# One transformer block in fp32 on one core: the two ends of the feed-forward rearranged, and the planner's estimate for one-pass products made shorter

## The chip, the cores and the metric

The kernel runs on one core of a Trainium2 chip. Its time is the device time of the whole program in microseconds (us). A core has engines that each take their instructions strictly in the order in which they were written: TensorE (PE in the profile, with its weight loads as PEld), VectorE (DVE), ScalarE (ACT), GpSimd (POOL), and queues that start DMA transfers (SP's above all). An engine waits on semaphores until what its next instruction reads is there, and everything behind that instruction waits too.

## The reference

One layer on 512 tokens of width 1024, all in fp32: a token mixer of four groups, attention to 256 memory rows, and a feed-forward of width 2816, each with a root-mean-square norm before it and another behind it.

```python
for l in range(DEPTH):                       # DEPTH = 1
    h = token_mixer(rmsnorm(x, norm_mix_pre[l]), ...)
    x = x + rmsnorm(h, norm_mix_post[l])
    h = memory_cross_attention(rmsnorm(x, norm_cross_pre[l]), rmsnorm(mem, mem_norm[l]), ...)
    x = x + rmsnorm(h, norm_cross_post[l])
    h = conv_glu_ffn(rmsnorm(x, norm_ffn_pre[l]), w_ffn_in[l], ffn_conv_w[l], ffn_conv_b[l], w_ffn_out[l])
    x = x + rmsnorm(h, norm_ffn_post[l])

def conv_glu_ffn(xn, w_up, conv_w, conv_b, w_down):
    gu = xn @ w_up
    gate, up = jnp.split(gu, 2, axis=-1)
    gate = causal_dwconv(gate, conv_w) + conv_b.astype(gate.dtype)
    return (jax.nn.silu(gate) * up) @ w_down
```

## The kernel before

**Products.** Each large fp32 product runs as three one-pass matmuls of a type called fp32r (`three`): high part by high part, low by high, high by low. `split` makes the parts: ScalarE copies the high part (`xTh`, `wh`, `sh`, `hh` ...), VectorE subtracts it from the value for the low part (`xTl`, `wl`, `sl`, `hl` ...). A "group" below is one such three of matmuls.

**Who orders the work.** Nothing is issued as the code is read. Every operation goes to a list scheduler (`Plan`), which knows a cost for it, what it depends on, and how many SBUF slots and PSUM banks (8) there are. It walks through an estimated time, takes the operation that can start first, and among those within 1 ns the one with the longest estimated rest of the program (`bl`) plus a `boost` written at the call. What comes out is one fixed list for each engine. The estimate for a matmul is `mcost`; it costs no time on the chip and acts only through the order.

**Feed-forward, first end.** After the attention to memory, each of four row tiles t of 128 tokens is normalized (`norm_T`: `xs` on VectorE, eight transposes on TensorE, then `xTh` and `xTl`). For t = 2 and 3 the transposed tile is also kept unsplit (`xf`, "keep"), and differences of kept tiles (t=2 with 0, 3 with 1) are split into `Th` and `Tl`.

**The 22 column tiles f.** The product with `w_ffn_in` is made for tiles of 128 gate and 128 up columns. Six tiles, `PLAIN`, are done by `plain`: two products of 8 groups, 512 columns wide. For f = 0 each product is made in two halves of 256 columns (tokens of t = 0, 1, and of t = 2, 3), so that the first halves need only row tiles 0 and 1. The other 16 are done by `seven`, a scheme with seven smaller products (S1, S3, G1, S2, S4, U2, G2) of 12 matmuls of 256 columns, on sums and differences of weight blocks made in `blocks` by VectorE (`su`, `st`) and split by ScalarE (`wh`, `uh`, `sh`) and VectorE (`wl`, `sl`, `ul`). Their results are put together again from the copies `c57`, `c1` (both named c in the rows) and `gu`; then `glu` (convolution, Silu, product) gives `hT`.

**Feed-forward, last end.** `hh` and `hl` are the parts of `hT` for the product with `w_ffn_out`. `down(f, t, c)` is one group of 512 columns; eight accumulators `od[t][c]` stand in all eight banks, and f runs in the outer loop, the last three f per row tile. What may not start before the end of the 22 tiles is tied to `up_`, the last tile's U2 product.

Of the kernel before, what the change touches and what calls it, by code (L numbers as in the profile page):

```python
# [22 lines left out]
AF = mybir.ActivationFunctionType  # L23
# [3 lines left out]
P = 128  # L27
S = 512
D = 1024
# [1 line left out]
NT = S // P  # L31
DFF = 2816
NF = DFF // P
PLAIN = (0, 1, 2, 6, 11, 16)
EPS = 1e-6
NEG = -1e30

# [305 lines left out]
def kernel(  # L343
# [108 lines left out]
    def mcost(l, n):  # L452
        m = min(l.size(), P)
        if l.buf.dt == FR:
            return max(n, 2 * m) * 0.4445 + 3.7
        return max(n, m) / 0.6 + 4.8

    def mms(o, terms, first=True, last=True, spare=0, n=None, quota=(), after=(), boost=0.0, fifo=None, cold=1, open_=False):
# [113 lines left out]
    @unit  # L572
    def norm_T(src, g, dst, keep=None):
        xs = [sb([P, 512], FT, "xs") for _ in range(2)]
        r = rms([src[:, h * 512:(h + 1) * 512] for h in range(2)], xs)
        for h in range(2):
            hs = slice(h * 512, (h + 1) * 512)
            stt(xs[h].all, src[:, hs], r[:, 0:1], g[:, hs], OP.mult, OP.mult)
        for h in range(2):
            p = ps([P, 4, P])  # L580
            for k in range(4):
                tpose(p[:, k, :], xs[h][:, k * P:(k + 1) * P], idn)
            if keep:
                act(keep[h], p.all, AF.Copy)
            split(*dst(h), p.all)

    def into(t):
        return lambda h: (xTh[:, t, 4 * h:4 * h + 4], xTl[:, t, 4 * h:4 * h + 4])
# [509 lines left out]
    for t in range(NT):  # L1098
        pl.boost = -5000.0 * t
        qh, ql = qT[t // 2]  # L1100
        tq = slice((t % 2) * P, (t % 2) * P + P)
        oh_, ol_ = sb([P, 4, P], FR, "oh"), sb([P, 4, P], FR, "ol")
        for hp in range(2):
            with pl.unit():
                sp, mx, pr = ps([P, 2, 256]), sb([P, 4], FT, "cmx"), sb([P, 2, 256], FT, "cpr")
                for hh in range(2):
                    h = hp * 2 + hh
                    mms(sp[:, hh, :], three(qh[:, h, tq], ql[:, h, tq], ckh[:, h, :], ckl[:, h, :]), n=256)
                rmax(mx[:, 0:2], sp.all)
                ts(mx[:, 0:2], mx[:, 0:2], -CS, None, OP.mult)  # L1110
                for hh in range(2):
                    act(pr[:, hh, :], sp[:, hh, :], AF.Exp, bias=mx[:, hh:hh + 1], scale=CS,
                        accum=mx[:, 2 + hh:3 + hh])
                recip(mx[:, 2:4], mx[:, 2:4])
                tt(pr.all, pr.all, mx[:, 2:4, None].bc([P, 2, 256]), OP.mult)
                tp, pt = ps([P, 2, 2, P]), sb([P, 2, 2, P], FT, "cpt")
                for hh in range(2):
                    for m in range(2):
                        tpose(tp[:, hh, m, :], pr[:, hh, m * P:(m + 1) * P], idn)
                act(pt.all, tp.all, AF.Copy)  # L1120
                oT = ps([P, 2, P])
                for hh in range(2):
                    h = hp * 2 + hh
                    mms(oT[:, hh, :], [(cv[:, m, h * P:(h + 1) * P], pt[:, hh, m, :]) for m in range(2)])
                split(oh_[:, 2 * hp:2 * hp + 2, :], ol_[:, 2 * hp:2 * hp + 2, :], oT.all)
        with pl.unit():
            pp = []
            for c in range(2):
                p, cs = ps([P, 512]), slice(c * 512, c * 512 + 512)
                for k in range(4):  # L1130
                    wh, wl = wo[k]
                    mms(p.all, three(oh_[:, k, :], ol_[:, k, :], wh[:, 0, cs], wl[:, 0, cs]), k == 0, k == 3,
                        spare=BIG)
                pp.append(p)
            xo2 = residual(pp, g_cpost, t)
        if t < 2:
            xf.append([sb([P, 4, P], FT, "xf") for h in range(2)])
            norm_T(X[t], g_fpre, into(t), [b.all for b in xf[t]])
        else:
            with pl.unit():  # L1140
                b1, b2 = [sb([P, 4, P], FT, "xf") for h in range(2)]
                norm_T(X[t], g_fpre, into(t), [b1.all, b2.all])
                a1, a2 = xf[t - 2]
                i = t - 2
                pl.boost -= 60000.0

                tt(a1.all, b1.all, a1.all, OP.subtract)
                tt(b1.all, b2.all, b1.all, OP.subtract)
                tt(b2.all, b2.all, a1.all, OP.subtract)
                tt(a2.all, a2.all, b2.all, OP.subtract)  # L1150
                for j, v in enumerate((a1, b2, b1, a2)):
                    split(Th[j][:, i], Tl[j][:, i], v.all)
                pl.boost += 60000.0
        kept.append(store(flat(x2, t * P * D, [[D, P], [1, D]]), X[t].all, P * D * 4))


# [18 lines left out]
    def plain(f):  # L1175
        ww = [stage(wsrc(w_ffn_in, 0, KT, j * DFF + f * P, P), [P, KT, P], 8 if f < 2 else 4) for j in range(2)]
        with pl.unit():
            pp = []
            for j in range(2):
                p = ps([P, S])  # L1180
                wh, wl = ww[j]
                for hv_ in [slice(0, 2), slice(2, 4)] if f < 1 else [slice(0, 4)]:
                    for k in range(KT):
                        o = mms(p[:, hv_.start * P:hv_.stop * P],
                                three(wh[:, k, :], wl[:, k, :], xTh[:, hv_, k, :], xTl[:, hv_, k, :]),
                                k == 0, k == KT - 1)
                pp.append(p)
            glu(f, pp[0], pp[1].all)
        return o

    def raw(f):
        with pl.unit():
# [48 lines left out]
    def seven(f):  # L1241
        W = blocks(*raw(f))
        with pl.unit():
            a, b = ps([P, 2, 256]), ps([P, 2, 256])

            def prod(o, w, xs, first):
                return mms(o, [q for i in range(4) for q in three(W[w][0][i], W[w][1][i], *xs[i])], first, n=256, open_=True)
            prod(b[:, 0], "S1", tblock(0), True)
            prod(b[:, 1], "S3", tblock(2), False)
            prod(a[:, 0], "G1", xblock(0, 0), True)  # L1250
            prod(a[:, 1], "S2", tblock(1), False)
            c57 = sb([P, 2, 256], FT, "c57")
            act(c57.all, b.all, AF.Copy)
            prod(b[:, 0], "S4", xblock(1, 1), False)
            o = prod(b[:, 1], "U2", tblock(3), False)
            c1 = sb([P, 256], FT, "c1")
            act(c1.all, a[:, 0], AF.Copy)
            prod(a[:, 0], "G2", xblock(1, 0), False)
# [4 lines left out]
            tt(c57[:, 0], c57[:, 0], c57[:, 1], OP.add)  # L1263
            tt(gu[:, 768:], c1.all, c57[:, 0], OP.add)
            glu(f, gu, gu[:, S:])
        return o

    ups = [plain(f) if f in PLAIN else seven(f) for f in range(NF)]
    up_ = ups[-1]

    g_fpost = gain(norm_ffn_post, [up_])
    NL = 3
    wd, hT = [], []
    for f in range(NF):
# [6 lines left out]
            wd.append((hb.all, lb2.all))  # L1281
        with pl.unit():
            hh, hl = sb([P, S], FR, "hh", kind="hh"), sb([P, S], FR, "hl")
            act(hh.all, hP[f // 2][:, f % 2, :], AF.Copy, quota=[("hh", 4)], after=[ups[-2]])
            tt(hl.all, hP[f // 2][:, f % 2, :], hh.all.cast(FT), OP.subtract)
            hT.append((hh, hl))

# [6 lines left out]
    od = [[ps([P, 512]) for c in range(2)] for t in range(NT)]  # L1294
    for t in range(NT):
        X[t] = sb([P, D], FT, "X2")
        load(X[t].all, flat(x2, t * P * D, [[D, P], [1, D]]), P * D * 4, after=[kept[t], up_])
    for f in range(NF - NL):
        with pl.unit():
            for t in range(NT):  # L1300
                for c in range(2):
# [121 lines left out]
```

## Time and profile before

| what | us |
|---|---|
| median of 3 runs | 748.5 (746.23 to 749.05) |
| the profiled execution | 747.11 |
| its span, first to last instruction | 745.3 |
| TensorE busy in it | 727.7 (98%) |
| VectorE busy | 522.6 (70%) |
| ScalarE busy | 389.1 (52%) |

The times are read on one profiled execution; start times in it are us from the span's start. TensorE's busy time counts overlapping matmuls by their union, so that a matmul listed with 0.39 us may start 0.23 us after the one before it: the distance between two starts is what one costs in a stream. In the rows, `[0.79 <-DVE xs L412]` behind an instruction says that its engine stood idle for 0.79 us before it and which engine's result ended that. The feed-forward's 22 tiles lie between 382 and 616 us, the product with `w_ffn_out` between 616 and 739 us.

### The profile page before, as it was taken

What the parts mean: (1) busy time and instruction counts of PE and PEld (TensorE: products, weight loads), DVE (VectorE), ACT (ScalarE), POOL (GpSimd) and SP (SyncE); (2) the same over time, 40 slices, a digit from 0 to 9 for tenths busy, and PEclk for the clock granted to TensorE, in tenths of its full rate; (3) what the DMA queues carried; (4) which work ended last, traced back from release to release, by engine and by line L of the source; (5) the groups of instructions that cost most, each with busy time, mean ns of one, the idle gap of its engine ahead of it and who ended that gap; (6) DMA issues with size and microseconds to landing.
All of it is one profiled execution on the core that took longest, in us unless ns stands there. A gap on an engine that the chain in (4) does not pass through costs nothing.

```text
span 745.3 us, 11908 instructions
## 1 busy us (share of the span) xinstructions
PE 727.7 (98%) x4614; PEld 647.4 (87%) x4614; DVE 522.6 (70%) x1007; ACT 389.1 (52%) x790; POOL 35.5 (5%) x65
## 2 busy tenths in 40 slices
PE   7999999999999999999999999999999989999996
PEld 6898989998887988889887999999999988888885
DVE  5889956785674646676888679898979997334105
ACT  6794347546574545465666355463655565324102
POOL 3000210011000001000010000000000000000001
PEclk9999999999999999999999999999999999999999
DMA  8800320410325543333134043052234146441003
GB/s 300 299 1 1 130 93 29 173 55 28 112 116 163 163 155 103 123 113 121 51 118 166 29 142 114 29 179 77 77 126 134 34 161 235 141 150 49 0 1 113
DMA packets 25696, 82.07 MB, mean 110 GB/s; under 512 B 2980, under 2 KB 4644, under 8 KB 25640
## 3 DMA queue, kind: packets, MB, share of 16 engines
q1 hardware_dynamic: 25352, 80.72, 31.9%
q8 instruction: 36, 0.59, 0.3%
q0 software_dynamic: 288, 0.59, 0.3%
q14 instruction: 20, 0.16, 0.1%
HBM read 77.10 MB, written 4.20 MB: 109 GB/s over the span
## 4 chain that ended last, share of the span: by engine, by line
PE 85%; DVE 7%; ACT 5%; issue 2%; DMA 1%; POOL 0%; SPq 0%; DVEq 0%; POOLq 0%; ACTq 0%
PE p L462 81%; PE p L479 3%; DMA st<-in_w_in_dram 1%; PE p L474 1%; ACT wh L387 1%; DVE at L428 1%; DVE wl L400 1%; DVE Qt L400 0%; ACT e L387 0%; POOL rr L565 0%; DVE xTl L400 0%; DVE X L412 0%; DVE pg L400 0%; DVE E L400 0%; DVE sl L400 0%
## 5 line engine op out<-in xcount | busy, mean ns | idle before, releaser
L462 PE MATMUL p<-xTh,wh 128*128 128x512 f32 (+1 forms) x432 | 147.4, 341 | 2.5 <-ACT c L387 2.0
L462 PE MATMUL p<-xTl,wh 128*128 128x512 f32 (+1 forms) x432 | 145.7, 337 | 0.7 <-DVE xTl L400 0.7
L462 PE MATMUL p<-xTh,wl 128*128 128x512 f32 (+1 forms) x432 | 145.3, 336 | 0.0
L400 DVE TENSOR_TENSOR wl<-st,wh 128x1024 fp32r<-128x1024 f32 (+3 forms) x101 | 118.7, 1190 | 29.8 <-ACT wh L387 29.7
L387 ACT ACTIVATE wh<-st 128x1024 fp32r<-128x1024 f32 (+3 forms) x101 | 101.5, 1029 | 8.5 <-DMA st<-in_w_in_dram 5.8
L462 PEld LDWEIGHTS p<-xTh,wh 128*128 128x128 f32 x432 | 81.7, 189 | 10.8 <-ACT c L387 2.4
L462 PEld LDWEIGHTS p<-xTh,wl 128*128 128x128 f32 x432 | 81.7, 189 | 9.3
L462 PEld LDWEIGHTS p<-xTl,wh 128*128 128x128 f32 x432 | 81.8, 189 | 8.4 <-DVE xTl L400 1.1
L462 PE MATMUL p<-wh,xTh 128*128 128x256 f32 (+1 forms) x192 | 56.5, 294 | 0.2 <-ACT xTh L387 0.2
L462 PE MATMUL p<-wh,hh 128*128 128x512 f32 x144 | 56.7, 394 | 0.0
L462 PE MATMUL p<-wh,hl 128*128 128x512 f32 x144 | 56.7, 394 | 0.0
L462 PE MATMUL p<-wl,hh 128*128 128x512 f32 x144 | 56.7, 394 | 0.0
L462 PE MATMUL p<-wh,xTl 128*128 128x256 f32 (+1 forms) x192 | 54.0, 281 | 0.4 <-DVE xTl L400 0.4
L462 PE MATMUL p<-wl,xTh 128*128 128x256 f32 (+1 forms) x192 | 54.1, 282 | 0.0
L462 PE MATMUL p<-Th,sl 128*128 128x256 f32 x192 | 54.0, 281 | 0.0
L462 PE MATMUL p<-Th,sh 128*128 128x256 f32 x192 | 53.9, 281 | 0.0
L462 PE MATMUL p<-Tl,sh 128*128 128x256 f32 x192 | 53.9, 281 | 0.0
L400 DVE TENSOR_TENSOR hl<-hT,hh 128x512 fp32r<-128x512 f32 x22 | 15.1, 690 | 52.8 <-ACT hh L387 52.8
L387 ACT ACTIVATE hh<-hT 128x512 fp32r<-128x512 f32 x22 | 13.8, 629 | 64.2 <-PE p L462 64.2
L565 POOL TENSOR_TENSOR rr<-rv,mhalf 128x1 f32<-128x1 f32 x26 | 15.8, 608 | 568.5 <-DVE rv L407 565.0
L462 PEld LDWEIGHTS p<-wh,xTh 128*128 128x128 f32 x192 | 36.2, 189 | 1.0 <-ACT xTh L387 0.5
L400 DVE TENSOR_TENSOR pg<-p,gain 128x512 f32<-128x512 f32 x24 | 16.4, 685 | 29.1 <-ACT sq L387 29.1
(281 smaller groups left out, 1760.9 us busy)
## 6 DMA issues: line engine op xcount, KB each, us to landing
st<-in_w_ffn_in_dram SPq DMA_DIRECT2D x44, 512.0 KB, 4.5
st<-in_w_in_dram SPq DMA_DIRECT2D x24, 512.0 KB, 4.3
st<-in_w_ffn_out_dram SPq DMA_DIRECT2D x22, 512.0 KB, 3.7
st<-in_w_mix_out_dram SPq DMA_DIRECT2D x8, 512.0 KB, 4.6
st<-in_w_ck_dram SPq DMA_DIRECT2D x4, 512.0 KB, 9.1
st<-in_w_cv_dram SPq DMA_DIRECT2D x4, 512.0 KB, 3.9
X<-in_x_dram SPq DMA_DIRECT2D x4, 512.0 KB, 3.9
st<-in_w_cq_dram SPq DMA_DIRECT2D x4, 512.0 KB, 3.9
```

The lines of the kernel that those rows point to most:

```text
L387: return nc.scalar.activation(o.ap(), i.ap(), func, **kw)
L400: return pl.op(eng, c, lambda: e.tensor_tensor(o.ap(), a.ap(), b.ap(), op=op), reads=[a, b], writes=[o], fifo=fifo, boost=boost)
L428: return pl.op("DVE", dcost(n, True), lambda: nc.vector.copy_predicated(o.ap(), m.ap(), a.ap()), reads=[m, a, o], writes=[o])
L462: i = nc.tensor.matmul(o.ap(), l.ap(), r.ap(), start=first and j == 0, stop=last and j == len(terms) - 1, skip_group_check=open_)
L474: i = nc.tensor.matmul(o[hh * 64:hh * 64 + 64].ap(), l.ap(), r.ap(), start=j == 0, stop=j == len(terms) - 1)
L479: return pl.op("PE", 109.0, lambda: nc.tensor.transpose(o.ap(), a.ap(), idn.ap()), reads=[a, idn], writes=[o])
L565: pl.op("Pool", 470.0, lambda: nc.gpsimd.tensor_tensor(r.all.ap(), v.all.ap(), mhalf[:, :1].ap(), op=OP.pow), reads=[v.all, mhalf.all], wr ...
```

## The change

- Of the six plain tiles, f = 16 becomes f = 17.
- `mcost` for fp32r goes from 231.3 to 215.7 ns for 512 columns and from 117.5 to 109.1 ns for 256 (the two formulas at n = 512 and 256): an estimate, which can only change orders.
- In `norm_T` the split is written ahead of the keep copy. The norm before the feed-forward gets a boost of 5000, and the differences of kept tiles one of -60000 alone.
- `plain` halves its products for f = 0 and f = 1. For f = 1 this takes away 16 groups of 512 columns and adds 32 of 256: 96 matmuls in place of 48.
- `plain` and `seven` return two operations. For the last tile these are its S1 product (`up_`) and its U2 product (`upe`). The `hh` copies wait for S1 of the last tile where they waited for the tile before it (U2 of f = 20); the gain and the loads of `X2` wait for U2 of the last tile as before.
- The eight `down` groups of f = 0 leave the common unit, become units of their own, and may start once S1 of the last tile is done.

```diff
-PLAIN = (0, 1, 2, 6, 11, 16)
+PLAIN = (0, 1, 2, 6, 11, 17)
...
         if l.buf.dt == FR:
-            return max(n, 2 * m) * 0.4445 + 3.7
+            return max(n, 2 * m) / 2.4 + 2.4
...
+            split(*dst(h), p.all)
             if keep:
                 act(keep[h], p.all, AF.Copy)
-            split(*dst(h), p.all)
...
+        pl.boost = 5000.0
         if t < 2:
...
-                pl.boost -= 60000.0
+                pl.boost = -60000.0
...
-                pl.boost += 60000.0
...
-                for hv_ in [slice(0, 2), slice(2, 4)] if f < 1 else [slice(0, 4)]:
+                for hv_ in [slice(0, 2), slice(2, 4)] if f < 2 else [slice(0, 4)]:
...
-            prod(b[:, 0], "S1", tblock(0), True)
+            o = prod(b[:, 0], "S1", tblock(0), True)
...
-            o = prod(b[:, 1], "U2", tblock(3), False)
+            e = prod(b[:, 1], "U2", tblock(3), False)
...
-        return o
+        return o, e
...
-    up_ = ups[-1]
-
-    g_fpost = gain(norm_ffn_post, [up_])
+    up_, upe = ups[-1]
+
+    g_fpost = gain(norm_ffn_post, [upe])
...
-            act(hh.all, hP[f // 2][:, f % 2, :], AF.Copy, quota=[("hh", 4)], after=[ups[-2]])
+            act(hh.all, hP[f // 2][:, f % 2, :], AF.Copy, quota=[("hh", 4)], after=[up_])
...
-        load(X[t].all, flat(x2, t * P * D, [[D, P], [1, D]]), P * D * 4, after=[kept[t], up_])
-    for f in range(NF - NL):
+        load(X[t].all, flat(x2, t * P * D, [[D, P], [1, D]]), P * D * 4, after=[kept[t], upe])
+    for t in range(NT):
+        for c in range(2):
+            down(od[t][c].all, 0, t, c)
+    for f in range(1, NF - NL):
```

How the planner then orders TensorE at the first end, between the transposes of row tile t = 2 and the first products of t = 2, 3 together. Before, the last of the 16 half groups of f = 0 stands directly ahead of the eight transposes of t = 3 (`ident,xs`), and the products behind them, f = 1 at 512 columns, read all four row tiles:

```order
2063 L462 MATMUL p_4361<-xTh_63,wl_3979 128x256
2064 L479 MATMUL p_4399<-ident_88,xs_4332 128x128 x4
2065 L479 MATMUL p_4407<-ident_88,xs_4365 128x128 x4
2066 L462 MATMUL p_4423<-xTh_63,wh_3989 128x512
2067 L462 MATMUL p_4423<-xTl_64,wh_3989 128x512
2068 L462 MATMUL p_4423<-xTh_63,wl_4003 128x512
```

In the changed order (`p_4398`, `p_4408` are the accumulators of the second product of each of f = 0 and f = 1, here in their first halves):

```order
2066 L462 MATMUL p_4408<-xTh_63,wh_4047 128x256
2067 L462 MATMUL p_4408<-xTl_64,wh_4047 128x256
2068 L462 MATMUL p_4408<-xTh_63,wl_4077 128x256
2069 L479 MATMUL p_4426<-ident_88,xs_4333 128x128 x4
2070 L462 MATMUL p_4398<-xTh_63,wh_3990 128x256
2071 L462 MATMUL p_4398<-xTl_64,wh_3990 128x256
2072 L462 MATMUL p_4398<-xTh_63,wl_4010 128x256
2073 L479 MATMUL p_4442<-ident_88,xs_4379 128x128 x4
2074 L462 MATMUL p_4408<-xTh_63,wh_4047 128x256
```

What moved: rows 2000 to 2068 of the changed order are 23 half groups where 16 stood, one more lies between the two fours of transposes, and rows 2074 to 2088 are five more, before row 2089 is the first that reads the row tiles t = 2, 3.

ScalarE at the last end, around the copy `c1` of the last tile but one, f = 20 (`c_1237`; `wh`, `uh`, `sh` belong to the weights of f = 21, `hh` to the product with `w_ffn_out`). Before:

```order
616 L387 ACTIVATE wh_6811<-st_6548 128x1024
617 L387 ACTIVATE uh_6815<-st_6550 128x512
618 L387 ACTIVATE hh_6817<-hT_5040 128x512
619 L387 ACTIVATE sh_6820<-su_6813 128x512
620 L387 ACTIVATE sh_6820<-st_6550 128x512
621 L387 ACTIVATE hh_6827<-hT_5040 128x512
622 L387 ACTIVATE c_1237_6831<-p_6753 128x256
623 L387 ACTIVATE sh_6835<-su_6822 128x512
```

In the changed order:

```order
611 L387 ACTIVATE fc_6813<-fc_6813,cols_254 128x512
612 L387 ACTIVATE c_1237_6846<-p_6785 128x256
613 L387 ACTIVATE wh_6849<-st_6596 128x1024
614 L387 ACTIVATE uh_6865<-st_6598 128x512
615 L387 ACTIVATE sh_6868<-su_6863 128x512
616 L387 ACTIVATE sh_6868<-st_6598 128x512
617 L387 ACTIVATE gu_6887<-p_6785 128x256
```

The copy `c1` now stands ahead of the whole weight chain of f = 21, and the first `hh` copy (row 622) behind that chain.

TensorE inside the last tile, f = 21 (`p_6920` and `p_6905` are its two banks, `p_6991` to `p_7080` the eight accumulators of the product with `w_ffn_out`). Before, all eight `down` groups of f = 0 follow the last tile's G2. In the changed order six of them stand ahead of G2, whose first row is 3724, and two behind U2:

```order
3721 L462 MATMUL p_7018<-wh_6898,hh_6933 128x512
3722 L462 MATMUL p_7018<-wl_6938,hh_6933 128x512
3723 L462 MATMUL p_7018<-wh_6898,hl_6970 128x512
3724 L462 MATMUL p_6920<-xTh_63,wh_6849 128x256
3725 L462 MATMUL p_6920<-xTl_64,wh_6849 128x256
3726 L462 MATMUL p_6920<-xTh_63,wl_6889 128x256
```

```order
3747 L462 MATMUL p_6905<-Th_4473,ul_6903 128x256
3748 L462 MATMUL p_7068<-wh_6898,hh_6933 128x512
3749 L462 MATMUL p_7068<-wl_6938,hh_6933 128x512
3750 L462 MATMUL p_7068<-wh_6898,hl_6970 128x512
3751 L462 MATMUL p_7080<-wh_6898,hh_6933 128x512
3752 L462 MATMUL p_7080<-wl_6938,hh_6933 128x512
```

What moved: six groups went between the products S4 and G2 of the last tile, and U2 went from ahead of G2 to behind it; the seventh and eighth group need the banks that the last tile itself held.

## Rows read from the trace of the kernel before

**Rows 1.** The page: busy time, share of the span and instructions of each engine.

```profile
PE 727.7 (98%) x4614; PEld 647.4 (87%) x4614; DVE 522.6 (70%) x1007; ACT 389.1 (52%) x790; POOL 35.5 (5%) x65
PE 85%; DVE 7%; ACT 5%; issue 2%; DMA 1%; POOL 0%; SPq 0%; DVEq 0%; POOLq 0%; ACTq 0%
```

**Rows 2.** TensorE's waits: for what, us in total, times, longest.

```profile
PE p L479 <- DVE xs L412: 3.8, 5, 1.1
PE p L462 <- ACT c L387: 2.0, 2, 1.5
PE p L462 <- DVE ol L400: 1.2, 1, 1.2
PE p L462 <- DVE xTl L400: 1.1, 2, 0.7
PE p L462 <- ACT xTh L387: 0.8, 2, 0.6
```

**Rows 3.** Timeline of TensorE, first end: start, us, operation [idle before].

```profile
381.74 1.04 PE L479 MATMUL p<-ident,xs 128*128 128x128 f32 x8
382.53 0.36 PE L462 MATMUL p<-xTh,wh 128*128 128x256 f32 x1
...
388.18 0.28 PE L462 MATMUL p<-xTh,wl 128*128 128x256 f32 x1
389.26 1.29 PE L479 MATMUL p<-ident,xs 128*128 128x128 f32 x8 [0.79 <-DVE xs L412]
391.12 0.50 PE L462 MATMUL p<-xTh,wh 128*128 128x512 f32 x1 [0.57 <-ACT xTh L387]
392.36 0.79 PE L462 MATMUL p<-xTl,wh 128*128 128x512 f32 x1 [0.74 <-DVE xTl L400]
392.95 0.63 PE L462 MATMUL p<-xTh,wl 128*128 128x512 f32 x1
393.38 0.63 PE L462 MATMUL p<-xTh,wh 128*128 128x512 f32 x1
...
395.63 0.28 PE L462 MATMUL p<-xTh,wh 128*128 128x256 f32 x1
```

**Rows 4.** Windows: busy us (and instructions) of each engine, granted clock, DMA share.

```profile
382.53:388.30 5.77, 5.77 (x51) 5.72 (x49) 5.39 (x11) 3.78 (x11) 2.05 (x2) 1.00 0.37 113
388.30:391.80 3.50, 1.92 (x11) 1.02 (x9) 3.40 (x6) 1.82 (x4) 0.03 (x1) 1.00 0.99 341
391.80:395.20 3.40, 2.84 (x7) 2.26 (x8) 3.40 (x6) 2.94 (x6) 0.00 (x0) 0.50 1.02 416
640.00:700.00 60.00, 60.00 (x260) 48.58 (x259) 22.41 (x23) 18.09 (x24) 0.00 (x0) 1.00 0.28 87
475.00:602.00 127.00, 127.00 (x961) 121.68 (x960) 116.03 (x186) 71.66 (x122) 0.00 (x0) 1.00 0.29 96
```

**Rows 5.** Timeline of VectorE, and one row of ScalarE, first end.

```profile
357.33 1.23 DVE L400 TENSOR_TENSOR wl<-st,wh 128x1024 fp32r<-128x1024 f32 x1 [0.50 <-ACT wh L387]
388.36 1.41 DVE L412 SCALAR_TENSOR_TENSOR xs<-X,rr,gain 128x512 f32<-128x512 f32 x2 [0.44 <-POOL rr L565]
391.62 1.28 DVE L400 TENSOR_TENSOR xTl<-p,xTh 128x512 fp32r<-128x512 f32 x2
390.48 0.59 ACT L387 ACTIVATE xTh<-p 128x512 fp32r<-128x512 f32 x1
```

**Rows 6.** Timelines of ScalarE, TensorE and VectorE, last end.

```profile
603.11 0.61 ACT L387 ACTIVATE hh<-hT 128x512 fp32r<-128x512 f32 x1
603.63 0.36 ACT L387 ACTIVATE c<-p 128x256 f32<-128x256 f32 x1
602.27 0.28 PE L462 MATMUL p<-Th,sl 128*128 128x256 f32 x1
604.04 0.39 PE L462 MATMUL p<-xTh,wh 128*128 128x256 f32 x1 [1.49 <-ACT c L387]
614.14 0.28 PE L462 MATMUL p<-Th,sl 128*128 128x256 f32 x1
614.90 0.39 PE L462 MATMUL p<-xTh,wh 128*128 128x256 f32 x1 [0.47 <-ACT c L387]
592.81 0.69 DVE L400 TENSOR_TENSOR sl<-su,sh 128x512 fp32r<-128x512 f32 x1
593.91 0.28 PE L462 MATMUL p<-Th,sh 128*128 128x256 f32 x1
```

**Rows 7.** Timeline of VectorE: where it waited inside the 22 tiles.

```profile
403.55 1.54 DVE L412 SCALAR_TENSOR_TENSOR fc<-p,cols,fc 128x511 f32<-128x511 f32 x2 [2.96 <-ACT fc L387]
425.62 0.43 DVE L400 TENSOR_TENSOR c<-c 128x256 f32<-128x256 f32 x1 [3.61 <-ACT c L387]
429.25 0.69 DVE L400 TENSOR_TENSOR gu<-c,p 128x512 f32<-128x512 f32 x1 [3.20 <-PE p L462]
475.89 0.42 DVE L400 TENSOR_TENSOR c<-c,p 128x256 f32<-128x256 f32 x1 [2.29 <-ACT gu L387]
```

More of the change, by code (lines that the diff above doesn't have):

```diff
@@ L1188, in plain @@
             glu(f, pp[0], pp[1].all)
-        return o
+        return o, o
     def raw(f):
@@ L1265, in seven @@
             glu(f, gu, gu[:, S:])
-        return o
+        return o, e
     ups = [plain(f) if f in PLAIN else seven(f) for f in range(NF)]
-    up_ = ups[-1]
-    g_fpost = gain(norm_ffn_post, [up_])
+    up_, upe = ups[-1]
+    g_fpost = gain(norm_ffn_post, [upe])
     NL = 3
```

## The prediction

> **What bounds the kernel.** I read the page first: TensorE is busy for 98% of the span and makes 85% of the chain that ended last; VectorE is busy for 70% [rows 1]. So time is won in two ways only: fewer or cheaper matmuls, or less waiting of TensorE. Then I read how fast TensorE runs when nothing stops it: 260 matmuls of 512 columns in 60 us at a granted clock of 1.00, which is 0.231 us from start to start [rows 4]; at 256 columns 48 matmuls of the first end lie between 382.53 and 388.30, 0.120 us each, and inside a stream one starts 0.118 behind the other, which I take [rows 3, 4]. The change adds almost no matmuls, so what counts is TensorE's list of waits [rows 2]: 3.8 us in five waits for a normalized tile (`xs`), 2.0 in two for the copy c, 1.2 for `ol`, 1.9 for `xTl` and `xTh`. The timelines show where they are. Three waits are at the first end, between 388 and 393 us [rows 3], the two for c at the last end [rows 6]. Between 475 and 602 us TensorE has no idle time at all, while VectorE is busy for 116.0 of 127 us [rows 4]: the second bound, near behind the first.
>
> **First end: the wait and the clock.** The last half group of f = 0 starts its third matmul at 388.18, so the next could start at 388.30. From there to 395.63 TensorE does eight transposes and nine 512-column matmuls [rows 3]. Eight transposes in the stream cost 0.79 (381.74 to 382.53), nine matmuls 9 × 0.231 = 2.08. So 7.33 − 0.79 − 2.08 = 4.46 us are lost. Of these 0.79 + 0.57 + 0.74 = 2.10 are the waits named in the rows; the rest is mostly the clock: in 391.80 to 395.20 the granted clock is 0.50, the lower level of 1.2 GHz, after a stretch in which TensorE was busy for 1.92 of 3.50 us [rows 4], and matmuls start 0.43 apart in place of 0.231 [rows 3], 7 × 0.2 = 1.4 us.
>
> The changed order puts 23 half groups where 16 stood between the transposes of t = 2 and those of t = 3. At 3 × 0.118 = 0.354 us a group TensorE is at the transposes of t = 3 at 382.53 + 23 × 0.354 = 390.67. Before, the first half of `xs` was there at about 389.1 (half of the two VectorE instructions from 388.36 that end at 389.77) [rows 5]; adding up, at their old durations, the instructions that now stand ahead of it on VectorE, I estimate 390.2, so 0.4 us to spare. Behind the transposes six more groups (2.1 us) stand ahead of the first product that reads row tile 3, and I put that at 382.53 + 29 × 0.354 + 0.79 = 393.6. `xTl` is the last that it needs; before it was ready about 3.6 us after the transposes' start (391.62 + 1.28 against 389.26) [rows 3, 5], now by the same addition at 393.35: 0.25 to spare. No wait of over 0.4 us and no drop of the clock is then left. The cover exists in time: the weights of f = 1, which the early groups need, are ready from about 358.6 [rows 5], 30 us ahead. I take 4.4 of the 4.46. Bounds: 4.46, and, if the clock drops all the same and the margins fail by 0.5 us each, 4.46 − 1.4 − 1.0 = 2.1.
>
> The price of the halves: 96 × 0.118 − 48 × 0.231 = 0.24 us, on TensorE and therefore on the path.
>
> The split ahead of the keep copy changes nothing where it would count: in the changed order ScalarE still copies the first `xf` of t = 3 ahead of the first `xTh`, since the planner's priorities and not the code's lines decide. Zero; at most one copy, 0.5 us, of a margin.
>
> **Last end.** TensorE loses 604.04 − 602.27 − 0.12 = 1.65 us before G2 of f = 20: it waits for the copy c1 on ScalarE, which stands behind two `hh` copies and the `sh` copies in the list. It loses 614.90 − 614.14 − 0.12 = 0.64 at the same place of f = 21 [rows 6]. Both go in the new order: the c1 of f = 20 stands ahead of the weight chain and the first `hh` behind it; G2 of f = 21 is covered by six `down` groups, 6 × 3 × 0.231 = 4.2 us. But two waits come up. With f = 17 the last plain tile, its spare groups are used up before f = 20, and f = 21 follows f = 20 directly: VectorE's chain from the copy c57 of f = 20 through `hT`, `su`, `wl` to the `sl` that S1 of f = 21 needs takes 10.9 us by the rows' durations, TensorE's seven products 84 × 0.118 = 9.9, so S1 waits about 1.0. And the eighth `down` group needs the bank from which VectorE reads `gu` of f = 21, behind a `wl` and an `hl`: about 0.95. The sum is 2.29 won, 1.95 lost: 0.3 won. Bounds: all of 2.3 won, or, if both new waits are twice as long, 1.6 lost.
>
> **The estimate in `mcost`.** It changes no instruction, but every order from 20 us on. Here two sources stand against each other. A stream on this chip shows 0.231 us at 512 columns, which is the old estimate; the new one is 6.7% below it [rows 4]. The Trainium skill, "TensorE: Matmul & The Clock Gate", section "Back-to-back issue gap", gives N/2.4 + 2.5 ns for an isolated matmul at full clock, 215.7 ns at 512 columns: that is the new value, and the measurement decides against it for this kernel; if matmuls really cost that here, an estimate worked out from the page would make the order more exact and the span no shorter by itself. With the short estimate the planner believes TensorE to be early: it thinks that products are finished sooner, and so places the VectorE and ScalarE instructions that read them too early in their lists. Outside the two ends I found rows moved by up to 26 us between 50 and 100 us and by a few us elsewhere, and the 1.2 us wait for `ol` at its place. I take 0; the bounds are the 2 us of waits that stand there (`ol` and a few of `xs`) as a gain and 3 us as a loss, an estimate: two or three waits as long as the longest in the list [rows 2].
>
> **Sum.** 747.1 − 4.4 + 0.2 − 0.3 = 742.6 for an execution like the profiled one. That one lies 1.4 below the median of the runs, 748.5, and 0.6 below the mean of all four executions; I add 0.6: **743.2 us**. With the bounds of the first end (2.1 us less won) and a small loss elsewhere it is 746, with the last end's full gain 741: its own range is 740.8 to 745.5.
>
> **The rivals.**
> *VectorE gives it back.* TensorE comes 4.4 us earlier into the 16 tiles of seven products, where VectorE has 11 us of idle time in 127 [rows 4] and the first `sl` of f = 20 is ready just 0.41 us before its S1 [rows 6]. If VectorE can't follow, S1 of some tiles waits until the lead is used up, and the time is 747.1 + 0.2 − 0.3 = 747.0, with the median's 0.6 747.6. For it: those margins. Against it: VectorE itself waited for results of TensorE, 2.96, 3.61, 3.20 and 2.29 us at 403, 425, 429 and 475 us [rows 7], 12 us in all; with TensorE earlier these shrink first, so the lead can pass through. Chance 0.22.
> *The first end is only half mended.* The tile t = 3 comes late all the same, or the granted clock falls in the new place: 1.4 to 2.4 us stay, 745.3. Chance 0.12. That the reordering there does not do what it says has this price too.
> *Slower.* In the tiles of seven products VectorE's list now holds instructions that wait for a product which TensorE, slower than estimated, has not finished: 84 × 0.0084 = 0.7 us a tile by the difference of the estimates (117.5 − 109.1 ns). VectorE stands there, and the next tile's `su`, `wl`, `sl` behind it come late. It has 11 us idle in about 12.8 tile times (127 / 9.9), 0.9 us a tile. So it decides only if the waits come to more than 0.9 a tile above those of now; at 1.5 TensorE loses 0.6 × 16 = 9.6 us: 743.2 + 9.6 = 752.8. For it: the estimate is wrong by that much in each tile. Against it: the error starts anew at each wait that the planner did not foresee. Chance 0.09.
>
> **Chances and range.** Forecast 0.57, VectorE 0.22, half mended 0.12, slower 0.09. A measurement of this kernel can tell about 0.5%, 3.7 us, from no change: faster is below 744.8, slower above 752.2. The forecast lies in part above 744.8 (0.1 of its 0.57), and the half-mended case in part below it (0.03); adding the chance that the orders elsewhere win up to 2 us, which brings 0.07 of the other cases across, I put faster at 0.57, same 0.35, slower 0.08. The range of 740.0 to 747.8 holds the forecast, its gains at both ends, the half-mended case and most of VectorE's; what is left out is the slower case and a tail, under 0.2.
>
> **What would show it.** Right: no wait for `xs`, `xTh` or `xTl` over 0.4 us behind 382 us, a granted clock of 1.00 there, first products of f = 0's second halves about 1.5 to 2 us earlier than 395.63; no idle time ahead of G2 of f = 20; a wait of about 1 us at S1 of f = 21 and one before the eighth `down` group. Wrong: waits of TensorE for `sl` or `wl` inside 400 to 600 us (VectorE), for `xTl` at 393 with the clock at 0.50 (half mended), or VectorE's waits for p growing tile by tile (slower). New waits over 2 us before 380 us, from the orders that I put at zero, would also make it wrong.

## The result and the profile after

The changed kernel takes 739.30 us (median of 4 runs, 738.95 to 739.74) against 748.54 (4 runs, 746.23 to 749.05): a ratio of 0.9887 with a 95% interval of 0.9867 to 0.9908. It is faster, as forecast, but by 9.2 us and not by 5.3, and 739.3 lies 0.7 us below the low end of the stated range. The profiled executions, 738.95 against 747.11, and their spans, 737.2 against 745.3, both differ by 8.1 to 8.2 us; those are the microseconds that the traces can place. Part of the spread of one kernel's times goes with TensorE's clock: of 17 executions of the kernel before on one chip, the five with a mean granted clock of 0.999 took 744.9 to 746.2 us, the three with 0.993 took 748.0 to 748.4.

The page of the changed kernel, busy time by engine and the chain that ended last by engine, answers to [rows 1]:

```profile
PE 723.8 (98%) x4662; PEld 648.5 (88%) x4662; DVE 522.4 (71%) x1007; ACT 391.8 (53%) x790; POOL 35.9 (5%) x65
PE 92%; DVE 4%; DMA 1%; issue 1%; ACT 1%; SPq 1%; POOL 0%; DVEq 0%; POOLq 0%; ACTq 0%
```

There are 48 more matmuls, and TensorE's part in the chain rises from 85% to 92%: less of the time is spent by other engines while TensorE waits. Its list of waits, to be read against [rows 2]:

```profile
PE p L479 <- DVE xs L412: 2.6, 3, 1.0
PE p L462 <- ACT xTh L387: 0.9, 1, 0.9
PE p L462 <- DVE gu L400: 0.8, 1, 0.8
PE p L462 <- DVE sl L400: 0.5, 1, 0.5
PE p L462 <- DVE xTl L400: 0.3, 1, 0.3
```

The waits for the copy c (2.0 us) and for `ol` (1.2) are gone, and what remains for `xs`, `xTh` and `xTl` lies in the first 20 us of the program. New are one wait for `gu` and one for `sl`. (Both lists leave out the wait for the first tile, `zero`, of 1.0 to 1.1 us at the program's start.)

The first end, timeline of TensorE, against [rows 3]:

```profile
378.16 1.03 PE L479 MATMUL p<-ident,xs 128*128 128x128 f32 x8
378.95 0.36 PE L462 MATMUL p<-xTh,wh 128*128 128x256 f32 x1
...
387.07 0.28 PE L462 MATMUL p<-xTh,wl 128*128 128x256 f32 x1
387.19 0.60 PE L479 MATMUL p<-ident,xs 128*128 128x128 f32 x4
387.55 0.36 PE L462 MATMUL p<-xTh,wh 128*128 128x256 f32 x1
...
387.99 0.60 PE L479 MATMUL p<-ident,xs 128*128 128x128 f32 x4
388.34 0.36 PE L462 MATMUL p<-xTh,wh 128*128 128x256 f32 x1
```

The eight transposes of row tile t = 3 now come in two fours with a half group between them, 8.24 us behind 378.95 (the prediction's 23 groups of 0.354 are 8.14), and no row waits. The windows, against [rows 4], columns as there:

```profile
388.60:392.00 3.40, 3.40 (x31) 3.40 (x31) 3.40 (x6) 2.91 (x6) 0.00 (x0) 1.00 1.02 411
392.00:395.40 3.40, 3.40 (x32) 3.40 (x31) 3.40 (x7) 2.22 (x3) 0.00 (x0) 1.00 1.02 414
630.00:690.00 60.00, 60.00 (x260) 48.54 (x259) 24.24 (x25) 20.26 (x25) 0.00 (x0) 1.00 0.32 97
```

TensorE is busy throughout at a granted clock of 1.00, where it stood at 0.50 before. The last row shows the stream's pace as it was: 260 matmuls of 512 columns in 60 us, 0.231 us each.

The last end, TensorE's two waits, against [rows 6]:

```profile
597.21 0.39 PE L462 MATMUL p<-Th,sl 128*128 128x256 f32 x1 [0.53 <-DVE sl L400]
612.86 0.47 PE L462 MATMUL p<-wh,hh 128*128 128x512 f32 x1 [0.84 <-DVE gu L400]
```

The first is inside S1 of f = 21, the second before the eighth `down` group. A matmul is listed for longer than the distance to the next start, so the loss by starts is some 0.17 us more than each listed wait.

What the result leaves open: TensorE reaches the first half group of f = 0 at 378.95, where it was at 382.53. These 3.6 us were won before either end begins. The only edits that reach so far up the program are the estimate and the boosts, through the order.

### The profile page after: what moved, and what is told of

Read it like the earlier page. It is cut to its first block, busy times and chain, and to the rows that moved or that the text cites. A ratio compares the mean times of both kernels' runs of the same rounds, so it can differ in the third digit from the quotient of the medians.

```text
span 737.2 us, 11994 instructions
## 1 busy us (share of the span) xinstructions
PE 723.8 (98%) x4662; PEld 648.5 (88%) x4662; DVE 522.4 (71%) x1007; ACT 391.8 (53%) x790; POOL 35.9 (5%) x65
## 4 chain that ended last, share of the span: by engine, by line
PE 92%; DVE 4%; DMA 1%; issue 1%; ACT 1%; SPq 1%; POOL 0%; DVEq 0%; POOLq 0%; ACTq 0%
PE p L462 88%; PE p L479 3%; DMA bbc<-in_b_in_dram 1%; PE p L474 1%; DVE at L428 1%; SPq L371 1%; DVE Qt L400 1%; DMA cols<-in_cols_dram 0%; DVE wl L400 0%; DVE X L412 0%; DVE E L400 0%; ACT sq L387 0%; DVE xs L412 0%; DVE su L400 0%; DVE xTl L400 0%
## 5 line engine op out<-in xcount | busy, mean ns | idle before, releaser
L462 PE MATMUL p<-xTh,wh 128*128 128x256 f32 (+1 forms) x448 | 149.5, 334 | 0.0
L462 PE MATMUL p<-xTl,wh 128*128 128x256 f32 (+1 forms) x448 | 147.6, 329 | 0.0
L462 PE MATMUL p<-xTh,wl 128*128 128x256 f32 (+1 forms) x448 | 147.4, 329 | 0.0
L462 PEld LDWEIGHTS p<-xTh,wl 128*128 128x128 f32 x448 | 84.3, 188 | 8.6
L462 PEld LDWEIGHTS p<-xTh,wh 128*128 128x128 f32 x448 | 84.4, 188 | 7.1 <-issue 0.3
L462 PEld LDWEIGHTS p<-xTl,wh 128*128 128x128 f32 x448 | 84.3, 188 | 6.6
L462 PEld LDWEIGHTS p<-wh,xTl 128*128 128x128 f32 x192 | 36.9, 192 | 0.5 <-DVE xTl L400 0.5
```

The source lines that it names most:

```text
L462: i = nc.tensor.matmul(o.ap(), l.ap(), r.ap(), start=first and j == 0, stop=last and j == len(terms) - 1, skip_group_check=open_)
```

## The experiments

Each expectation stands as it was written before the run. "Ratio" is to the kernel before, over the same chip's runs, with the 95% interval.

**The estimate alone, and everything but the estimate.**

```diff
 the kernel before, with only
-            return max(n, 2 * m) * 0.4445 + 3.7
+            return max(n, 2 * m) / 2.4 + 2.4
```

> The kernel before with only the shorter estimate in mcost. Theory 1: the 3.3 us that the changed kernel is ahead before 380 us come from the orders that the shorter estimate makes; then this kernel reaches the end of the attention to memory about 3.3 us earlier than the kernel before, keeps the waits of about 4.4 us at the first end and 2.6 us at the last, and takes 743.8 us against 747.1 profiled (ratio about 0.9955). Theory 2 (rival): the estimate is worth nothing by itself and the 3.3 us come with the boosts and the other edits, since these change the length of the rest of the program by which the planner chooses; then the time is within 1 us of the kernel before.

Measured: 743.44 us, ratio 0.9955 (0.9936 to 0.9974); the profiled execution 742.65 against 747.11. Its first end has the waits of the kernel before (0.80, 0.57 and 0.73 us for `xs`, `xTh` and `xTl`), but in this execution the granted clock stayed at 1.00 behind them:

```profile
384.00:387.40 3.40, 1.86 (x10) 1.02 (x9) 3.35 (x6) 1.77 (x4) 0.00 (x0) 1.00 0.99 366
387.40:390.80 3.40, 2.79 (x14) 2.35 (x15) 3.40 (x6) 3.01 (x6) 0.00 (x0) 1.00 1.03 419
```

The same matmuls there take 6.15 us by their starts (383.82 to 389.97) where the kernel before took 7.45 (388.18 to 395.63). So 1.3 of the 4.46 us that the kernel before lost at the first end were the clock, and of the 4.5 us between the two profiled executions 1.3 came up at this place and not ahead of it.

```diff
 the changed kernel, with
-            return max(n, 2 * m) / 2.4 + 2.4
+            return max(n, 2 * m) * 0.4445 + 3.7
```

> The changed kernel with the old estimate in mcost. Theory 1: it loses the 3.3 us before 380 us (waits of about 1.8 us more at 50 to 100 us, 0.7 at 133, 1.1 at 333) and keeps the gain at the first end, 742.3 us against 739.0 profiled. Theory 2: it is within 1 us of the changed kernel.

Measured: 742.82 us, ratio 0.9946 (0.9929 to 0.9963), against 0.9887 for the changed kernel: 0.6% of it, some 4.4 us, gone. Both runs are those of theory 1, within the noise. The stretch from 25 to 360 us, which ends before the feed-forward, shows it. The window of the kernel before (columns as above: TensorE's busy time and matmuls come first):

```profile
25.00:360.00 335.00, 332.51 (x2124) 292.99 (x2123) 234.18 (x551) 189.67 (x432) 22.07 (x35) 1.00 0.31 104
```

That of the changed kernel:

```profile
25.00:360.00 335.00, 334.60 (x2151) 296.21 (x2149) 237.38 (x558) 194.87 (x443) 22.76 (x34) 1.00 0.31 104
```

That of the kernel before with the new estimate alone:

```profile
25.00:360.00 335.00, 334.55 (x2151) 296.21 (x2150) 236.72 (x558) 193.46 (x443) 22.76 (x34) 1.00 0.30 103
```

And that of the changed kernel with the old estimate:

```profile
25.00:360.00 335.00, 332.50 (x2127) 293.15 (x2126) 235.16 (x552) 191.67 (x434) 22.11 (x35) 1.00 0.31 103
```

TensorE's idle time in it is 2.49 and 2.50 us with the old estimate, 0.40 and 0.45 with the new one, and 24 to 27 matmuls more are begun in the same 335 us. The same by work and not by time: from one `wl,xTh` matmul at 24.05 us (24.33 in the changed kernel) to the end of the transposes of row tile t = 2, the same matmuls in both. The kernel before and the changed kernel:

```profile
24.05:382.51 358.46, 355.97 (x2269) 313.36 (x2268) 252.08 (x588) 207.46 (x481) 24.26 (x39) 1.00 0.30 102
24.33:378.93 354.60, 353.96 (x2269) 313.03 (x2268) 252.64 (x589) 208.06 (x480) 24.96 (x38) 1.00 0.30 102
```

That is 3.9 us less; with the estimate alone (24.05 to 378.15) it is 4.4 us less. Idle time makes 1.9 and 2.0 us of it. The rest is starts that lie closer together, nearly all among the matmuls of up to 128 columns: by their starts and without idle time these 592 take 71.7 us before, 70.0 in the changed kernel and 69.4 with the estimate alone. What held them apart before is not settled.

How a wait goes is seen where `ra`, a small result of VectorE, was waited for. Timeline of TensorE in the kernel before:

```profile
132.28 0.40 PE L462 MATMUL p<-xTh,wl 128*128 128x512 f32 x1
132.52 0.28 PE L462 MATMUL p<-wh,xTh 128*128 128x256 f32 x1
...
133.11 0.28 PE L462 MATMUL p<-wh,xTl 128*128 128x256 f32 x1
134.04 0.22 PE L479 MATMUL p<-ident,ra 4*128 4x4 f32 x1 [0.65 <-DVE ra L400]
```

and the kernel before with the new estimate alone:

```profile
130.25 0.40 PE L462 MATMUL p<-xTh,wl 128*128 128x512 f32 x1
130.48 0.28 PE L462 MATMUL p<-wh,xTh 128*128 128x256 f32 x1
...
131.76 0.28 PE L462 MATMUL p<-wh,xTl 128*128 128x256 f32 x1
131.97 0.22 PE L479 MATMUL p<-ident,ra 4*128 4x4 f32 x1
```

Before, 6 matmuls of 256 columns stand between the wide stream and the transposes that need `ra`; now 12, and the result is there in time. The reading that fits this place: a planner that takes the matmuls for shorter believes that TensorE runs out of independent work sooner, and lays more of it ahead of a matmul that has to wait.

**Other lengths of the estimate, and a margin put elsewhere.** Was this luck, as any reshuffle of the lists might have brought?

```diff
 the changed kernel, with
-            return max(n, 2 * m) / 2.4 + 2.4
+            return (max(n, 2 * m) * 0.4445 + 3.7) * 1.05
 or * 0.97, or * 0.90
```

> The changed kernel with the estimate at 105% of the old one (4.5 to 5% above what a stream shows). Theory M, margin: a shorter estimate makes the planner believe that TensorE is through with its independent groups sooner, so it puts more of them ahead of a matmul that needs another engine's result, and a longer one fewer. Then the waits for ol (1.2 us) and ra (0.7 us) that the old estimate has are back or longer, and the time is 743 to 746, no better than with the old estimate (742.8). Theory L, lottery: any other estimate reshuffles the lists and the 3.4 us were luck; then there is no order, and this one may lie anywhere from 739 to 745.

> The changed kernel with the estimate at 97% of the old one, about half of the change. Theory M: about half of the 3.5 us, 740.5 to 742, one of the waits for ol and ra gone or both shorter. Theory L: no relation.

> The changed kernel with the estimate at 90% of the old one, below the new one (93.3%). Theory M: the waits for ol and ra stay away, the first half group of f = 0 starts no later than in the changed kernel (378.95), and the time is 737.5 to 739.5, unless VectorE's lists get so far out of step that it stalls. Theory L: again anywhere from 739 to 745.

```diff
 the changed kernel, with the old estimate, and
     LAT = {...
+           ("DVE", "PE"): 500.0, ("ACT", "PE"): 500.0}
 (200.0 for these two by default)
```

> The changed kernel with the old, accurate estimate for matmuls, but 300 ns more assumed between a result of VectorE or ScalarE and the matmul that reads it. Theory M: it is the margin that counts and not the matmul's length, so this alone takes the waits for ol and ra away and the time is 738.5 to 741. Theory L, or a theory that the length of the matmuls acts through the ranking of the rest of the program: 742 to 744, as with the old estimate.

Measured; the idle time is that of TensorE from 25 to 360 us, 335 less the busy time, and the count that of the matmuls begun there:

| estimate | time, us | ratio | idle, us | matmuls |
|---|---|---|---|---|
| 105% of the old | 752.64 | 1.0063 (1.0048 to 1.0078) | 5.71 | 2106 |
| 100% | 742.82 | 0.9946 (0.9929 to 0.9963) | 2.50 | 2127 |
| 97% | 742.50 | 0.9929 (0.9913 to 0.9946) | 1.31 | 2139 |
| 93.3% (the change) | 739.30 | 0.9887 (0.9867 to 0.9908) | 0.40 | 2151 |
| 90% | 742.29 | 0.9922 (0.9907 to 0.9936) | 0.37 | 2151 |
| 100%, 300 ns more to TensorE | 744.54 | 0.9952 (0.9937 to 0.9967) | 2.62 | 2138 |

The window of the kernel at 105%:

```profile
25.00:360.00 335.00, 329.29 (x2106) 290.53 (x2105) 231.36 (x546) 187.89 (x429) 21.29 (x35) 1.00 0.31 104
```

That of the kernel at 90%:

```profile
25.00:360.00 335.00, 334.63 (x2151) 296.15 (x2150) 238.19 (x560) 194.94 (x444) 20.90 (x34) 1.00 0.30 104
```

Ahead of the feed-forward the idle time falls in step with the estimate, which a lottery would hardly do; there theory M fits all five values. At the last end there is no such order: TensorE's listed waits at S1 of f = 21 and in the first `down` groups add up to 2.5 us at 105%, 1.1 at 100%, 2.5 at 97%, 1.4 at 93.3% and 3.1 at 90%. So the whole time follows the estimate only in part, and theory M's expectations for 97% and 90% were missed by 0.5 and 3 us. Two lines of TensorE's waits in the kernel at 90% show where its time goes:

```profile
PE p L462 <- DVE gu L400: 1.9, 1, 1.9
PE p L462 <- DVE sl L400: 1.7, 2, 1.2
```

Of these 3.6 us, 3.1 stand at the two places of the last end where the changed kernel waits 1.4, and 0.5 inside the 16 tiles. Behind them the granted clock was 0.50 from 616.7 to 620.1 us, with matmuls of 512 columns 0.43 us apart. That a too short estimate gets VectorE's lists out of step, as the prediction's slower rival has it, is not shown: the kernel at 105%, whose estimate errs the other way, waits longer for `sl`, 2.8 us. That kernel came out some 7 us slower than either theory expected; it is 7.6 us behind the changed kernel already before the first end. The run with 300 ns more refutes the simple form of theory M. The waits for `ol` and `ra` did go from their places, but others came, idle time stayed at 2.62 us, and the time is that of the old estimate. So a fixed margin on every result that TensorE reads does not do what the shorter length of all matmuls did. Why is not settled, and with it theory M's mechanism stays a reading that fits and not one that is shown.

**The first end: halves and boosts.** The split ahead of the keep copy needed no run. With the two lines swapped back, the changed kernel's lists are the same on every engine, row by row.

```diff
 the changed kernel, with
-                for hv_ in [slice(0, 2), slice(2, 4)] if f < 2 else [slice(0, 4)]:
+                for hv_ in [slice(0, 2), slice(2, 4)] if f < 1 else [slice(0, 4)]:
```

> The changed kernel with f = 1 done in one piece of 512 columns again. If the halves of f = 1 are what mends the first end, TensorE waits again for xs, xTh and xTl of row tile 3, the granted clock falls to 0.50 for some 3 us there, and the time goes up by 4.4 - 0.2 = 4.2 us to 743.1. Rival: the boosts for the norm bring row tile 3 earlier by themselves; then no more than 2 us come back and the clock stays at 1.00.

Measured: 744.47 us, ratio 0.9959 (0.9944 to 0.9974), 5.2 us above the changed kernel. Its first end, timeline of TensorE:

```profile
386.38 1.29 PE L479 MATMUL p<-ident,xs 128*128 128x128 f32 x8 [1.59 <-DVE xs L412]
388.24 0.80 PE L462 MATMUL p<-xTh,wh 128*128 128x512 f32 x1 [0.57 <-ACT xTh L387]
389.35 0.80 PE L462 MATMUL p<-xTl,wh 128*128 128x512 f32 x1 [0.32 <-DVE xTl L400]
```

And two windows of it:

```profile
385.00:388.50 3.50, 1.52 (x9) 1.10 (x9) 3.50 (x6) 2.42 (x5) 0.25 (x1) 0.96 0.99 331
388.50:392.00 3.50, 3.18 (x7) 2.18 (x8) 3.50 (x7) 2.59 (x6) 0.00 (x0) 0.50 1.01 411
```

The waits and the low clock are back, so the boosts alone mend nothing. More came back than expected: the wait for `xs` is 1.59 us where it was 0.79 in the kernel before, and the clock was at 0.50 for 6.8 us (388.2 to 395.1) where it was for 3.4. I took the halves for the cause, and tried them alone.

```diff
 the kernel before, with only
-                for hv_ in [slice(0, 2), slice(2, 4)] if f < 1 else [slice(0, 4)]:
+                for hv_ in [slice(0, 2), slice(2, 4)] if f < 2 else [slice(0, 4)]:
```

> The kernel before with only the halves of f = 1. If the prediction's first term stands by itself, the waits for xs, xTh and xTl behind the transposes of row tile 3 go and the granted clock stays at 1.00 there: 747.1 - 4.4 + 0.2 = 742.9 us, ratio about 0.9945. Rival: the halves need the boosts (without them VectorE brings row tile 3 later) and half of the loss stays: 745, ratio about 0.997.

Measured: 749.82 us, ratio 1.0030 (1.0016 to 1.0044): slower than the kernel before, against both expectations. Its first end, timeline of TensorE:

```profile
394.10 1.03 PE L479 MATMUL p<-ident,xs 128*128 128x128 f32 x8
396.42 0.38 PE L462 MATMUL p<-xTh,wh 128*128 128x256 f32 x1 [1.29 <-ACT xTh L387]
397.57 0.39 PE L462 MATMUL p<-xTl,wh 128*128 128x256 f32 x1 [0.77 <-DVE xTl L400]
```

Two windows of it:

```profile
393.40:396.80 3.40, 2.11 (x17) 1.68 (x15) 1.27 (x2) 2.01 (x5) 0.00 (x0) 1.00 1.03 413
396.80:400.20 3.40, 2.63 (x15) 2.63 (x15) 3.40 (x7) 1.73 (x4) 0.00 (x0) 0.69 0.65 265
```

And one line of TensorE's waits:

```profile
PE p L462 <- ACT c L387: 2.9, 2, 2.4
```

The wait for `xs` has gone, but all 32 half groups now stand ahead of the transposes and none behind them, so TensorE waits for `xTh` and `xTl` instead, and the clock is at 0.50 in part of the next stretch (398.1 to 401.5). At the last end the wait for c has grown from 2.0 to 2.9 us, in lists that the same edit reshuffled, and there the clock was at 0.50 behind it as well (606.3 to 609.7), which it was not in the kernel before. So the 749.82 us are not the first end's alone. Then the changed kernel without the boosts:

```diff
 the changed kernel, with
-        pl.boost = 5000.0
         if t < 2:
...
-                pl.boost = -60000.0
+                pl.boost -= 60000.0
...
+                pl.boost += 60000.0
```

> The changed kernel without its two changes of boost. If the halves alone mend the first end, no wait over 0.4 us behind the transposes of row tile 3 and a time within 0.7 us of the changed kernel (ratio 0.988 to 0.990). Rival: the boosts carry a part; then 1 to 4 us are lost again at the first end, with a wait for xs (ratio 0.990 to 0.994).

Measured: 741.46 us, ratio 0.9921 (0.9896 to 0.9945), 2.2 us above the changed kernel: the rival in its loss, though it waits for `xTh` and `xTl` and not for `xs`. The intervals still touch; the place shows it. Its waits are those of the halves alone (1.29 us for `xTh`, 0.76 for `xTl`), but here the clock stayed at 1.00 behind them:

```profile
389.40:392.80 3.40, 2.03 (x16) 1.59 (x14) 1.36 (x3) 2.10 (x5) 0.00 (x0) 1.00 1.03 413
392.80:396.20 3.40, 2.72 (x23) 2.73 (x24) 3.40 (x7) 1.63 (x3) 0.00 (x0) 1.00 0.58 235
```

So two edits work together: the halves give the work, and the boost raises the norm, transposes included, above part of that work, so that nine of the 32 half groups are left to stand behind the first four transposes. It is the boost of 5000 that does it: with that one alone the planner's lists are those of the changed kernel on every engine, and with only the change to -60000 they are those of the kernel without boosts.

**The last end.**

```diff
 the changed kernel, with the first kernel's last end:
-    up_, upe = ups[-1]
+    up_ = upe = ups[-1][1]
...
-            act(hh.all, ..., after=[up_])
+            act(hh.all, ..., after=[ups[-2][1]])
...
-    for t in range(NT):
-        for c in range(2):
-            down(od[t][c].all, 0, t, c)
-    for f in range(1, NF - NL):
+    for f in range(NF - NL):
```

> The changed kernel with the last end tied as before: the hh copies wait for U2 of f = 20, all eight down groups of f = 0 for U2 of f = 21. By the prediction's sum the rearrangement itself trades waits of 2.3 us for waits of 2.0; undone, the wait of 1.0 us before the eighth down group goes, waits for c1 before the G2 of f = 20 or 21 come back (0.6 to 2.3 us), and the time stays within 1 us of 739.0. Rival: the rearrangement carries more than it seems, and 2 us or more are lost without it.

Measured: 739.48 us, ratio 0.9903 (0.9876 to 0.9929): within 1 us of the changed kernel, as expected, though the waits for c are back, as its timeline of TensorE shows:

```profile
596.41 0.39 PE L462 MATMUL p<-xTh,wh 128*128 128x256 f32 x1 [1.89 <-ACT c L387]
607.21 0.39 PE L462 MATMUL p<-xTh,wh 128*128 128x256 f32 x1 [0.47 <-ACT c L387]
```

That is 2.4 us of waits in place of 1.4. Two kernels then aimed at these 1.4.

```diff
 the changed kernel, with
+    for f in range(2):
     for t in range(NT):
         for c in range(2):
-            down(od[t][c].all, 0, t, c)
+            pl.boost = -4000.0 if t == NT - 1 else 0.0
+            down(od[t][c].all, f, t, c)
...
-            after=[up_] if f == 0 else [])
+            after=[up_] if f == 0 else [upe, upg] if f == 1 else [])
 and in the second kernel also
-PLAIN = (0, 1, 2, 6, 11, 17)
+PLAIN = (0, 1, 2, 6, 11, 19)
```

Here `upg` is the last tile's G2 product, which `seven` returns as a third operation.

> The changed kernel with the first two f of the down groups as units of their own: those of f = 1 wait for the last tile's U2 and G2, and the groups of the last row tile come with a boost of -4000, so that 12 groups (8.3 us) stand between the last tile and the first group that needs its banks. If the wait of 1.0 us before the eighth down group is what the prediction took it for (a bank that VectorE still reads), it goes: 1.0 us faster than the changed kernel, 738.0 against 739.0. Rival: the down groups no longer cover c1 of the last tile, and 0.6 us or more come back before its G2.

> The same with f = 19 in place of f = 17 as the last plain tile, so that its spare groups lie between f = 20 and f = 21. If S1 of f = 21 waits because f = 21 follows f = 20 directly, this wait of 0.7 us goes too: 1.7 us faster than the changed kernel, 737.3. Rival: VectorE gets the waits back at an earlier tile, since its work for f = 17 and 18 now lies in a row with others: no better than the kernel with 17.

Measured: 738.47 us with 17, ratio 0.9877 (0.9854 to 0.9900); 739.22 with 19, ratio 0.9888 (0.9867 to 0.9910). TensorE's only wait at the last end, with 17:

```profile
598.41 0.39 PE L462 MATMUL p<-Th,sl 128*128 128x256 f32 x1 [0.53 <-DVE sl L400]
```

And with 19:

```profile
598.98 0.38 PE L462 MATMUL p<-Th,sl 128*128 128x256 f32 x1 [1.66 <-DVE sl L400]
```

With 17 the wait for the bank is gone and no other came. The whole time can't show it: in this execution the first transposes waited 1.5 us longer for their data than in the changed kernel's (2.38 against 0.90 us), and the intervals overlap. So it is no slower than the changed kernel, and its gain of 1 us is shown at its place only. With 19 the wait for `sl` before S1 of f = 21 grew from 0.53 to 1.66 us: no better than with 17, as the rival had it, though at the same place and not at an earlier tile. The spare groups are not what this wait lacks.

## Why the prediction was right or wrong

**The bound and the first end: right in size, incomplete in cause.** TensorE's waits were what there was to win. Between the two profiled executions the first end gave back the 4.4 us: transposes 8.24 us behind the first half group where 8.14 was worked out, no wait of over 0.4 us, clock at 1.00. But the prediction costed the halves and named the order that came of them, and it never asked which edit made that order. The boosts have no term in it. The runs show that without them the halves leave 2.2 us of the gain behind in the changed kernel, and all of it in the kernel before. It also counted the low clock as a part of what these waits cost. The kernel with the estimate alone has the same waits at a clock of 1.00 and loses 1.3 us less, so that the 4.4 are the gain over an execution in which the clock fell.

**The price of the halves** (0.24 us) is under what these runs can show. **The swap of split and keep** was rightly put at nothing.

**The last end: right in mechanism, and nearly in size.** The waits for c, 2.29 us by starts, went. In their place S1 of f = 21 loses 0.70 us (1.0 was worked out) and the eighth `down` group 1.01 (0.95); both come by the distance between the starts of neighbours in the stream, less 0.12 and 0.23 for the matmul itself. So 0.6 us were won in place of 0.3 by the traces. Undoing the rearrangement left the time within 0.2 us of the changed kernel's.

**The estimate: the step that failed.** "I take 0; the bounds are the 2 us of waits that stand there ... as a gain and 3 us as a loss." Ahead of the first end it is worth 3.9 us in the changed kernel's trace, counted from 24 us on (3.6 from the start, since the clock happened to be at 0.50 from 10.8 to 14.2 us in that execution), and 4.4 in the trace of the kernel with this edit alone. Over the whole time it is worth 3.4 us as the only edit (0.45%, interval 1.9 to 4.8). Two things were wrong. The direction was argued from one side: that consumers on VectorE and ScalarE come too early in their lists. The other side of the same error, that TensorE gets more independent work ahead of a matmul that must wait, was left out; the runs fit it ahead of the feed-forward, where idle time falls with the estimate at all five values. And the upper bound counted only waits that the list names: 1.9 us of idle time went, and 2.0 us more came from starts that lie closer together, which no list of waits shows. With this term at 3.6 and the last end at 0.6 the sum is 747.1 − 4.4 + 0.2 − 0.6 − 3.6 = 738.7, and the profiled execution took 738.95: nothing else of size is left to explain. That 93.3% came out best of the five values is partly luck, since the waits at the last end follow no order with the estimate. In the trace after, matmuls of 512 columns still start 0.231 us apart, so the new estimate of 215.7 ns is not more exact; it helped by being too short. The Trainium skill, "TensorE: Matmul & The Clock Gate", section "Back-to-back issue gap", gives N/2.4 + 2.5 ns for an isolated matmul, the new estimate within 0.1 ns, and about 131 ns for a sustained stream at 512 columns; this kernel's stream shows neither.

**The rivals.** VectorE did not give the lead back: the only wait for `sl` in the changed kernel is the 0.53 us at f = 21. The half-mended case is what the kernel without boosts shows. The slower case did not come at 93.3%, and no run shows its mechanism: at 90% all but 0.5 us of the 3.6 us of waits for `sl` and `gu` lie at the last end.

**A slip in the sum.** For its upper end the prediction writes "2.1 us less won" at the first end; by its own working 2.1 us is what would still be won there, 2.3 less than 4.4. It changes no reading here.

## What to carry to other kernels

A planner's cost is worth what the order it makes is worth, not what it gets right: try a few values around the measured one, and look at each stage apart, since the same value that fills TensorE in one stage can lengthen the waits of another. Work added to cover a wait must also be placed: cover that all stands ahead of the first of two dependent steps only moves the wait to the second. When a change is an order, ask of each edit what the order is without it before giving one of them the whole gain.

## What the runs showed of the hardware

At the first end the granted clock of TensorE was 0.50 behind stretches in which it had been busy for 1.92 of 3.50 us and 1.52 of 3.50 us, and in part (0.69 on the mean of 3.40 us) behind one of 2.11 of 3.40. But it stayed at 1.00 behind 1.86 of 3.40 us (the estimate alone) and 2.03 of 3.40 us (no boosts), so a stretch with such waits does not settle by itself whether the clock falls, and what settles it these runs do not show. In the changed kernel, busy throughout, it stayed at 1.00 there. While it is low, matmuls of 512 columns start 0.43 us apart in place of 0.231; at the first end of the kernel before that was 1.3 of the 4.46 us lost.
